# Rotating keys and queries straight from PSUM, with the head norm's factor applied afterwards on GpSimd

## The chip, the cores and the metric

One core of one Trainium2 chip. The metric is device time in microseconds of one execution of the kernel, from its start to its end. A profiled execution gives a trace besides: busy time of TensorE (PE, with its weight loads as PEld), VectorE (DVE), ScalarE (ACT), GpSimd (POOL) and the DMA queue of SyncE (SP).

## What is computed

One transformer block over 1024 latent tokens and 256 context tokens, 1024 wide: norm and modulation, a state-space branch, an attention branch with 16 query heads and 4 key/value heads of 64, a merge, and a squared-ReLU MLP. The part that matters here makes keys and queries: a projection, an RMS norm over the 64 columns of each head, the norm's weight, and a rotation by the token's row and column.

```python
def rms_norm(x, g):
    xf = x.astype(jnp.float32)
    xf = xf * lax.rsqrt(jnp.mean(xf * xf, axis=-1, keepdims=True) + NORM_EPS)
    return xf.astype(x.dtype) * g
...
q_l = apply_axial_rope(rms_norm(p_l[..., OFF_Q:OFF_K].reshape(bsz, n_tok, N_HEADS, HEAD_DIM), q_norm_g[l]), cos, sin)
k_l = apply_axial_rope(rms_norm(p_l[..., OFF_K:OFF_V].reshape(bsz, n_tok, N_KV_HEADS, HEAD_DIM), k_norm_g[l]), cos, sin)
...
k_c = rms_norm(_cols(p_c, c0, OFF_K, OFF_V).reshape(bsz, n_ctx, N_KV_HEADS, HEAD_DIM), k_norm_g[l])
```

In the rotation, the two halves of 16 columns of each axis are mixed: `x1 * cos - x2 * sin` and `x2 * cos + x1 * sin`. The norm's factor is one number for a token and a head, so it may stand before or after the rotation. Context keys (`k_c`) have no rotation.

## The kernel before

Tokens are cut into ten tiles of 128: tiles 0 to 7 latent, 8 and 9 context. Every product is made in near-float32 precision from operands split in two: `wtile` (line 124) loads a weight tile over SyncE's queue (three raw buffers), makes its high half on ScalarE (line 135) and its low half on GpSimd (line 136), with four buffers for each half. `units` (line 200) multiplies one or two token tiles with the four weight tiles of a chunk, three matmuls for each of eight pieces of the contraction (lines 210 to 212), and the third reads the low half. Its output is a PSUM tile `mm` (three buffers) or, in the wide form, alternately `mm` and `s` (three more).

The stage at issue follows the state-space branch. Keys and values come first, in the order of tiles 0 and 1 together, 2, 3, 8, 9, 4 and 5, 6 and 7 (line 1019). Then come the queries in two halves of 512 columns (eight heads each, line 1109): tiles 0 and 1 together, 2, 3, 4, 5, and 6 and 7, together in the first half and one by one in the second. Last are the values of tiles 4 to 7 (line 1131), whose place in `Vt` had been used for keys. Between the units of the second query half stand the row maxima of the first attention step (lines 1086 and 1088), two calls after each unit.

`norm_rope` (line 965) takes the PSUM tiles of one call, one or two of them. ScalarE squares each (line 974, one buffer), VectorE sums the squares by head (line 975), then makes the inverse root in a chain of 11 small operations (line 977 and `rsqrt`, lines 149 to 153), on 4, 8 or 16 columns, once for the call. Then, tile by tile, VectorE multiplies the PSUM tile with the factor into `qn` in SBUF (line 983), and makes from `qn` a product with the cosines (line 991) and two with the sines (line 996, into `t1`, one buffer). GpSimd adds the two (line 997). Context keys take one product with the norm's weight instead (line 987). The cosine and sine tables already hold the weight. After `norm_rope`, query tiles are stored to DRAM (line 1115) and read back transposed by column blocks in `qprep`; key tiles are transposed on TensorE in `k_prep` (line 1009).

In this stage no order is written out by hand: a planner orders the instructions of each engine by program order and by when it expects their inputs, and each engine's queue runs in that order. From line 1291 on, attention has a handwritten order for TensorE, VectorE, ScalarE and GpSimd.

Of the kernel before, what the change touches and what calls it, by code (L numbers as in the profile page):

```python
# [8 lines left out]
F32 = mybir.dt.float32  # L9
# [3 lines left out]
OP = mybir.AluOpType  # L13
AX = mybir.AxisListType
# [6 lines left out]
NH, NKV, HD = 16, 4, 64  # L21
# [3 lines left out]
EPS = 1e-6  # L25
# [23 lines left out]
def block_kernel(ctx, tc, io, out, dbg=None):  # L49
    nc = tc.nc  # L50
    V, S, G, T = nc.vector, nc.scalar, nc.gpsimd, nc.tensor
    LD = nc.sync
# [94 lines left out]
    def rsqrt(y, v, tmp):  # L147

        V.tensor_scalar(y.bitcast(I32), v.bitcast(I32), -0.5, 1597463007.0, op0=OP.mult, op1=OP.add)
        for _ in range(3):  # L150
            V.tensor_tensor(tmp, y, y, op=OP.mult)
            V.scalar_tensor_tensor(tmp, tmp, -0.5, v, op0=OP.mult, op1=OP.mult)
            V.scalar_tensor_tensor(y, tmp, 1.5, y, op0=OP.add, op1=OP.mult)
# [5 lines left out]
    sq = sq_.__enter__()  # L159
# [3 lines left out]
    def mmb():  # L163
        return psA.tile([128, 512], F32, name="mm", tag="mm", bufs=3)

    def six():

        cnt["n"] ^= 1
        return mmb() if cnt["n"] else psA.tile([128, 512], F32, name="s", tag="s", bufs=3)

    def trb():
        return psA.tile([128, 512], F32, name="tr", tag="tr", bufs=2)
# [12 lines left out]
    def h_l(t, k):  # L185

        f, i = (t // 4, t % 4) if t < 8 else (2, t - 8)
        return hH[f, k][:, i * 128:(i + 1) * 128], hL[f, k][:, i * 128:(i + 1) * 128]

    def chunk(c0, mid=None):  # L190

        ws = []
        for kp in range(4):
            if kp == 3 and mid:
                mid()
            src = w_in[kp * 256:(kp + 1) * 256, c0:c0 + 512].rearrange("(a p) n -> p a n", p=128)
            ws.append(wtile(src, (2, 512)))
        return ws

    def units(ws, ts, n=512, wide=False):  # L200

        pss = [(six() if wide else mmb()) for _ in ts]
        per = 8 // len(ws)
        w = 1024 // per
        for k in range(8):
            wH, wL = ws[k // per]
            o = slice((k % per) * w, (k % per) * w + n)
            for ps, t in zip([ps[:, :n] for ps in pss], ts):
                lH, lL = h_l(t, k)
                T.matmul(ps, lH, wH[:, o], start=k == 0, stop=False)  # L210
                T.matmul(ps, lL, wH[:, o], start=False, stop=False)
                T.matmul(ps, lH, wL[:, o], start=False, stop=k == 7)
        return pss
# [204 lines left out]
    for q in range(4):  # L418
# [5 lines left out]
        if q == 0:  # L424
# [6 lines left out]
            p = trb()  # L431
            for i in range(3):
# [12 lines left out]
                            op=OP.mult)  # L445
# [163 lines left out]
    for nm in ("re", "im"):  # L609
        craw = pm.tile([128, 2, 2, 128], F32, name="craw" + nm)  # L610
        src = io["ssm_c_" + nm][0].rearrange("d (o q r) h p -> d o q h r p", o=2, r=2)
# [7 lines left out]
    for nm in ("re", "im"):  # L619
        p = trb()  # L620
# [9 lines left out]
    for nm in ("re", "im"):  # L630
        b = st.tile([128, 512], F32, name="hf", tag="hf", bufs=4).rearrange("p (n h) -> p n h", h=GH)
        src = io["ssm_b_" + nm][0].rearrange("d (q r) p h -> (r p) (d q) h", r=2)
# [110 lines left out]
    for g8 in range(0, NG, 16):  # L743
        p = trb()
# [151 lines left out]
    for c in range(2):  # L896
        src = io["w_glu"][0][:, c * 256:(c + 1) * 256].rearrange("(a p) n -> p a n", p=128)
# [6 lines left out]
    for f in range(2):  # L904
        yf, gH, gL = [], [], []
        for c in range(4):
            p = trb()
            for t in range(4):
                T.transpose(p[:, t * 128:(t + 1) * 128], yld[4 * f + t][:, c * 128:(c + 1) * 128], ident)
            a = yp.tile([128, 512], F32, name="yf", tag="yf", bufs=4)  # L910
            h = yp.tile([128, 512], F32R, name="ygH", tag="ygH", bufs=5)
# [7 lines left out]
        for c in range(4):  # L919
            ps = mmb()  # L920
            wH, wL = wg[c // 2]
            prs = []
            for k in range(4):
                o = k * 256 + (c % 2) * 128
# [36 lines left out]
    rp = rp_.__enter__()  # L961
    gk = rp.tile([128, 64], F32, name="gk")
    tab = rope_tab(gk, "k_norm_g")

    def norm_rope(us, nh):

        n = nh * 64
        m = nh * len(us)
        vv = rp.tile([128, 16], F32, name="vv", tag="vv", bufs=2)[:, :m]
        yy = rp.tile([128, 16], F32, name="yy", tag="yy", bufs=2)[:, :m]  # L970
        tt = rp.tile([128, 16], F32, name="tt", tag="tt", bufs=2)[:, :m]
        for i, (ps, t, o) in enumerate(us):
            sq = rp.tile([128, 512], F32, name="sq", tag="sq", bufs=1)
            S.activation(sq[:, :n], ps[:, :n], AF.Square)
            V.tensor_reduce(vv[:, i * nh:i * nh + nh], sq[:, :n].rearrange("p (h d) -> p h d", d=64), axis=AX.X,
                            op=OP.add)
        V.tensor_scalar(vv, vv, 1.0 / HD, EPS, op0=OP.mult, op1=OP.add)
        rsqrt(yy, vv, tt)
        sh = [128, nh, 64]
        for i, (ps, t, o) in enumerate(us):  # L980
            qn = rp.tile([128, 512], F32, name="qn", tag="qn", bufs=2)
            qv = qn[:, :n].rearrange("p (h d) -> p h d", d=64)
            V.tensor_tensor(qv, ps[:, :n].rearrange("p (h d) -> p h d", d=64),
                            yy[:, i * nh:i * nh + nh, None].to_broadcast(sh), op=OP.mult)
            ov = o.rearrange("p (h d) -> p h d", d=64)
            if t >= 8:
                V.tensor_tensor(ov, qv, gk[:, None, :].to_broadcast(sh), op=OP.mult)
                continue
            cs_, sn_ = tab
            t1 = rp.tile([128, 512], F32, name="t1", tag="t1", bufs=1)  # L990
            V.tensor_tensor(ov, qv, cs_[:, t:t + 1, :].to_broadcast(sh), op=OP.mult)
            for h in range(2):
                src = qn[:, :n].rearrange("p (h a i) -> p h a i", a=2, i=32)[:, :, :, 16 * (1 - h):16 * (1 - h) + 16]
                dst = t1[:, :n].rearrange("p (h a i) -> p h a i", a=2, i=32)[:, :, :, 16 * h:16 * h + 16]
                sv = sn_[:, t:t + 1, :].rearrange("p o (a i) -> p o a i", i=32)[:, :, :, 16 * h:16 * h + 16]
                V.tensor_tensor(dst, src, sv.to_broadcast([128, nh, 2, 16]), op=OP.mult)
            G.tensor_tensor(o, o, t1[:, :n], op=OP.add)

    ws = chunk(1024)
    ksb = {}  # L1000

    def k_prep(tiles):

        c0 = tiles[0] * 128
        n = 128 * len(tiles)
        for pr_ in range(2):
            p = trb()
            for i, t in enumerate(tiles):
                T.transpose(p[:, i * 128:(i + 1) * 128], ksb[t][:, pr_ * 128:(pr_ + 1) * 128], ident)
            w = slice(c0, c0 + n)  # L1010
            ha, hb = 2 * pr_, 2 * pr_ + 1
            S.activation(KH[ha][0:64, w], p[0:64, :n], AF.Copy)
            S.activation(KH[ha][64:128, w], p[0:64, :n], AF.Copy)
            V.tensor_tensor(K2[ha][0:64, w], p[0:64, :n], KH[ha][0:64, w], op=OP.subtract)
            S.activation(KH[hb][64:128, w], p[64:128, :n], AF.Copy)
            S.activation(KH[hb][0:64, w], p[64:128, :n], AF.Copy)
            V.tensor_tensor(K2[hb][0:64, w], p[64:128, :n], KH[hb][64:128, w], op=OP.subtract)

    for ts in ([0, 1], [2], [3], [8], [9], [4, 5], [6, 7]):
        late = ts[0] in (4, 6)  # L1020
        us = []
# [20 lines left out]
    rp = rp_.__enter__()  # L1042
    gq = rp.tile([128, 64], F32, name="gq")
    tab = rope_tab(gq, "q_norm_g")
    q_d = dr.tile([8, 128, 1024], F32, name="q_d")
# [63 lines left out]
    for n in range(2):  # L1109
        ws = chunk(512 * n)  # L1110
        for ts in ([0, 1], [2], [3], [4], [5], [6, 7]) if n == 0 else ([0, 1], [2], [3], [4], [5], [6], [7]):
            us = [(ps, t, rp.tile([128, 512], F32, name="qo", tag="qo", bufs=2)) for ps, t in zip(units(ws, ts, wide=n == 0), ts)]
            norm_rope(us, 8)
            for _, t, qo in us:
                LD.dma_start(q_d[t][:, 512 * n:512 * n + 512], qo)
            if n == 0 and ts == [3]:
                k_prep((4, 5, 6, 7))
            if n == 0 and ts == [6, 7]:
                list(qprep(0))
                ms, fin = maxima(0)  # L1120
            if n == 1 and ms:
                for _ in range(2):
                    ms.pop(0)()
                if not ms:
                    list(fin())
                    list(qprep(1))
    ws = []
    for kq in range(2):
        src = w_in[kq * 512:(kq + 1) * 512, 1280:1536].rearrange("(a p) n -> p a n", p=128)
# [223 lines left out]
    def mmc():  # L1353
        return psC.tile([128, 512], F32, name="mm", tag="mm", bufs=6)
# [109 lines left out]
    def w_out_tile(n, kp):  # L1464
        src = io["w_out"][0][kp * 256:(kp + 1) * 256, n * 512:(n + 1) * 512].rearrange("(a p) n -> p a n", p=128)
        return wtile(src, (2, 512), scale_row=g1row[:, n * 512:(n + 1) * 512])
# [118 lines left out]
    for n in range(2):  # L1585
        ws = [w_out_tile(n, kp) for kp in range(4)] if n else ws_o
        for ts in ([0, 1], [2], [3], [4], [5], [6, 7]):
            pss = [mmc() for _ in ts]
            for k in range(8):
                wH, wL = ws[k // 2]  # L1590
                o = slice((k % 2) * 512, (k % 2) * 512 + 512)
# [161 lines left out]
    for bi, fts in enumerate(BL):  # L1753
        last_ = bi == NBL - 1
        tiles = (pre, pre2)[bi] if bi < 2 else [mlp2_tiles(ft) for ft in fts]
        for t in range(8):
# [4 lines left out]
            for n in range(2):  # L1761
                o = slice(n * 512, (n + 1) * 512)
                ps = mmc()
# [42 lines left out]
```

## Time and profile before

| | us |
|---|---|
| three runs, lowest, median, highest | 1907.51, 1910.69, 1912.46 |
| the profiled execution, time | 1909.88 |
| its span, first to last instruction | 1908.2 |
| TensorE busy | 1841.1 (96%) |
| VectorE busy | 1279.1 (67%) |
| GpSimd busy | 895.4 (47%) |
| ScalarE busy | 691.9 (36%) |

The time holds some 1.7 us around the span. The mean granted clock of TensorE is 0.985 of full speed. Shares over the whole span mix stages with different limits, so what a change in one stage is worth is read from that stage: from its stretch of time, and from the wait that ends last in it. The stage of keys, queries and values lies between 425 and 590.7 us.

### The profile page before, as it was taken

The numbers are of one execution on the slowest core, as the hardware profiler recorded it, in microseconds if no ns is written. First come the engines' busy times: TensorE is split into PE (matmuls) and PEld (weight loads), VectorE is DVE, ScalarE is ACT, GpSimd is POOL, SyncE is SP. The second block draws the span as 40 slices with busy tenths as digits, with TensorE's granted clock in tenths as the row PEclk, the third lists the DMA queues.
The fourth block names the chain that finished last, engine by engine and source line by source line (L and its number), as shares of the span: only waits on it lengthen the run. The fifth ranks groups of instructions, "written<-read, shape, count | busy, mean of one in ns | idle before, by whom it ended". The sixth has DMA issues, their size and how long they took to land. (4 is left out here: it accounts for less than half of the span.)

```text
span 1908.2 us, 25109 instructions
## 1 busy us (share of the span) xinstructions
PE 1841.1 (96%) x9250; PEld 1402.6 (74%) x9250; DVE 1279.1 (67%) x2194; ACT 691.9 (36%) x1016; POOL 895.4 (47%) x471
## 2 busy tenths in 40 slices
PE   7889999998999999999989999999999999999998
PEld 4668888887776556556547777887888877878887
DVE  5989998738897787777645455486454457545556
ACT  4542222244314555555442121455444541111110
POOL 2232333313425777777784453375444564443330
PEclk9989999999999999999999999999999999999999
DMA  9412222221222000000006664355554465333213
GB/s 308 97 56 71 76 77 78 76 85 46 84 71 78 18 23 23 23 23 18 22 13 207 213 209 144 116 177 182 155 155 152 126 218 178 110 107 104 89 55 144
DMA packets 179339, 200.72 MB, mean 105 GB/s; under 512 B 28112, under 2 KB 128260, under 8 KB 179216
## 3 DMA queue, kind: packets, MB, share of 16 engines
q1 hardware_dynamic: 179216, 199.11, 32.6%
q8 instruction: 73, 1.20, 0.3%
q14 instruction: 50, 0.41, 0.1%
HBM read 154.85 MB, written 44.09 MB: 104 GB/s over the span
## 5 line engine op out<-in xcount | busy, mean ns | idle before, releaser
L1202 POOL TENSOR_TENSOR accP<-accP,P 128x1024 f32<-128x1024 f32 x96 | 240.9, 2510 | 20.9 <-ACT P L1184 15.7
L1766 DVE TENSOR_TENSOR acc<-acc,mm 128x512 f32<-128x512 f32 x240 | 162.5, 686 | 127.6 <-PE mm L145 127.6
L136 POOL TENSOR_TENSOR wL<-wr,wH 128x1024 fp32r<-128x1024 f32 (+1 forms) x58 | 135.9, 2351 | 197.9 <-ACT wH L135 187.0
L1184 ACT ACTIVATE P<-sT 128x1024 f32<-128x1024 f32 x160 | 163.8, 1026 | 116.6 <-PE sT L1180 114.1
L1088 DVE TENSOR_REDUCE m<-mx 128x1 f32<-128x512 f32 x240 | 154.5, 686 | 76.1 <-PE mx L1086 69.7
L143 PE MATMUL mm<-wH,sH 128*128 128x512 f32 x480 | 187.3, 390 | 1.3 <-DVE acc L1766 1.2
L144 PE MATMUL mm<-wL,sH 128*128 128x512 f32 x480 | 186.8, 389 | 0.0
L145 PE MATMUL mm<-wH,sL 128*128 128x512 f32 x480 | 186.7, 389 | 0.0
L1197 PE MATMUL pv<-P,Vt 128*64 128x512 f32 x640 | 150.5, 600 | 0.0
L1738 POOL TENSOR_TENSOR sL<-wr,sH 128x1024 fp32r<-128x1024 f32 x30 | 72.2, 2406 | 152.0 <-ACT sH L1737 152.0
L135 ACT ACTIVATE wH<-wr 128x1024 fp32r<-128x1024 f32 (+1 forms) x62 | 61.9, 1005 | 216.2 <-PE mm L144 96.4
L1737 ACT ACTIVATE sH<-wr 128x1024 fp32r<-128x1024 f32 x30 | 31.6, 1054 | 226.5 <-issue 160.7
L1177 PE MATMUL sT<-Q,KH 128*128 128x512 f32 x320 | 105.3, 410 | 2.2 <-ACT P L1184 2.2
L143 PEld LDWEIGHTS mm<-wH,sH 128*128 128x128 f32 x480 | 90.1, 188 | 22.5 <-DVE acc L1766 2.9
L145 PEld LDWEIGHTS mm<-wH,sL 128*128 128x128 f32 x480 | 90.1, 188 | 18.9
L144 PEld LDWEIGHTS mm<-wL,sH 128*128 128x128 f32 x480 | 90.1, 188 | 18.2
L143 PE MATMUL mm<-hH,wH 128*128 128x512 f32 x248 | 101.1, 408 | 0.0
L1180 PE MATMUL sT<-Q,K 65*128 65x512 f32 x320 | 100.9, 396 | 0.0
L145 PE MATMUL mm<-hH,wL 128*128 128x512 f32 x248 | 97.7, 394 | 0.0
L144 PE MATMUL mm<-hL,wH 128*128 128x512 f32 x248 | 97.3, 392 | 0.0
L1197 PEld LDWEIGHTS pv<-P,Vt 128*64 128x64 f32 x640 | 41.7, 136 | 71.6 <-issue 62.3
L1666 POOL TENSOR_TENSOR wL<-wr,wH 128x1024 fp32r<-128x1024 f32 x32 | 76.8, 2405 | 36.6 <-ACT wH L1665 36.6
(581 smaller groups left out, 4722.8 us busy)
## 6 DMA issues: line engine op xcount, KB each, us to landing
wr<-in_w_mlp_dram SPq DMA_DIRECT2D x48, 512.0 KB
wr<-in_w_in_dram SPq DMA_DIRECT2D x35, 512.0 KB
wr<-in_w_mod_dram SPq DMA_DIRECT2D x32, 512.0 KB
s_d<-r SPq DMA_DIRECT2D x64, 256.0 KB
wr<-s_d SPq DMA_DIRECT2D x32, 512.0 KB
rw<-in_w_mlp_dram SPq DMA_DIRECT2D x30, 512.0 KB
x<-in_x_dram SPq DMA_DIRECT2D x12, 512.0 KB
xt<-in_w_mod_dram SPq DMA_DIRECT2D x24, 256.0 KB
```

The lines of the kernel that those rows point to most:

```text
L136: (low or G).tensor_tensor(L[:, :n], raw[:, :n], H[:, :n], op=OP.subtract)
L143: T.matmul(ps, lH, rH, start=i == 0, stop=False)
L144: T.matmul(ps, lH, rL, start=False, stop=False)
L145: T.matmul(ps, lL, rH, start=False, stop=i == n - 1)
L1088: V.tensor_reduce(m3[:, 4 * j + t, c:c + 1], m, axis=AX.X, op=OP.max)
L1177: T.matmul(o, KH[kv][:, ks], Q1[:, j], start=True, stop=False)
L1180: T.matmul(o, K2[kv][:, ks], Q2[:, j], start=False, stop=True)
L1184: S.activation(P, sT, AF.Exp, scale=HD ** -0.5)
L1197: T.matmul(pv[64 * j:64 * j + 64, :], Vt[:, kt, kv * 64:kv * 64 + 64], P[:, j * 512:(j + 1) * 512], start=kt == 0, stop=kt == NK - 1)
L1202: G.tensor_tensor(accP, accP, P, op=OP.add)
L1666: (low or G).tensor_tensor(L[:, :n], raw[:, :n], H[:, :n], op=OP.subtract)
L1766: V.tensor_tensor(a_, a_ if bi else bb2[:, o], ps, op=OP.add)
```

## The change

It stands in `norm_rope` and its two callers. The rotation's three products, and the one product of context keys, read the PSUM tile itself; `qn` and the pass that made it are gone. The sums of squares go into a list `pend` that is kept between calls; when it holds two token tiles, one chain makes both inverse roots, and GpSimd multiplies each rotated tile with its factor, in place. So tiles that come one by one wait for the next one. A query tile's store is issued after that multiplication. `t1` has two buffers in place of one, `qo` four in place of two.

```diff
-    def norm_rope(us, nh):
+    pend = []
+
+    def norm_rope(us, nh, done=None):
+
         n = nh * 64
-        m = nh * len(us)
-        vv = rp.tile([128, 16], F32, name="vv", tag="vv", bufs=2)[:, :m]
...
-        for i, (ps, t, o) in enumerate(us):
+        sh = [128, nh, 64]
+        for ps, t, o in us:
+            if not pend:
+                pend.append(rp.tile([128, 16], F32, name="vv", tag="vv", bufs=2))
+            i = len(pend) - 1
+            pend.append((o, t))
             sq = rp.tile([128, 512], F32, name="sq", tag="sq", bufs=1)
             S.activation(sq[:, :n], ps[:, :n], AF.Square)
-            V.tensor_reduce(vv[:, i * nh:i * nh + nh], ...)
+            V.tensor_reduce(pend[0][:, i * nh:i * nh + nh], ...)
-        V.tensor_scalar(vv, vv, 1.0 / HD, EPS, op0=OP.mult, op1=OP.add)
-        rsqrt(yy, vv, tt)
-        sh = [128, nh, 64]
-        for i, (ps, t, o) in enumerate(us):
-            qn = rp.tile([128, 512], F32, name="qn", tag="qn", bufs=2)
-            qv = qn[:, :n].rearrange("p (h d) -> p h d", d=64)
-            V.tensor_tensor(qv, ps[:, :n].rearrange("p (h d) -> p h d", d=64),
-                            yy[:, i * nh:i * nh + nh, None].to_broadcast(sh), op=OP.mult)
+            qv = ps[:, :n].rearrange("p (h d) -> p h d", d=64)
...
-            t1 = rp.tile([128, 512], F32, name="t1", tag="t1", bufs=1)
+            t1 = rp.tile([128, 512], F32, name="t1", tag="t1", bufs=2)
             V.tensor_tensor(ov, qv, cs_[:, t:t + 1, :].to_broadcast(sh), op=OP.mult)
             for h in range(2):
-                src = qn[:, :n].rearrange(...)
+                src = ps[:, :n].rearrange(...)
...
             G.tensor_tensor(o, o, t1[:, :n], op=OP.add)
+        if len(pend) < 3:
+            return
+        m = 2 * nh
...
+        V.tensor_scalar(vv, vv, 1.0 / HD, EPS, op0=OP.mult, op1=OP.add)
+        rsqrt(yy, vv, tt)
+        for i, (o, t) in enumerate(pend[1:]):
+            ov = o.rearrange("p (h d) -> p h d", d=64)
+            G.tensor_tensor(ov, ov, yy[:, i * nh:i * nh + nh, None].to_broadcast(sh), op=OP.mult)
+            if done:
+                done(o, t)
+        pend.clear()
...
-            us = [(ps, t, rp.tile([128, 512], F32, name="qo", tag="qo", bufs=2)) for ps, t in ...]
-            norm_rope(us, 8)
-            for _, t, qo in us:
-                LD.dma_start(q_d[t][:, 512 * n:512 * n + 512], qo)
+            us = [(ps, t, rp.tile([128, 512], F32, name="qo", tag="qo", bufs=4)) for ps, t in ...]
+            norm_rope(us, 8, lambda o, t: LD.dma_start(q_d[t][:, 512 * n:512 * n + 512], o))
```

## Rows read from the trace of the kernel before

**Rows 1.** Busy us by stretch, instructions in brackets; then clock, DMA share, GB/s.

```profile
480.00:513.50 33.50, 33.50 (x155) 27.82 (x154) 30.32 (x80) 11.42 (x17) 12.89 (x12) 1.00 0.17 62
513.50:530.00 16.50, 12.73 (x45) 9.98 (x44) 15.00 (x31) 3.81 (x6) 8.22 (x4) 0.79 0.42 128
530.00:580.00 50.00, 44.36 (x205) 35.31 (x205) 46.79 (x127) 9.59 (x16) 16.16 (x10) 0.98 0.23 80
580.00:590.70 10.70, 10.70 (x73) 10.70 (x74) 6.44 (x20) 0.77 (x2) 2.59 (x2) 0.78 0.59 195
sum 165.70, PE 150.38 PEld 125.02 DVE 141.33 ACT 49.12 POOL 57.89; mean PE 30.08 PEld 25.00 DVE 28.27 ACT 9.82 POOL 11.58
...
640.00:960.00 320.00, 319.52 (x1435) 188.48 (x1432) 246.26 (x328) 175.30 (x215) 235.19 (x101) 1.00 0.08 22
```

**Rows 2.** TensorE's waits, 425 to 595 us: total us, times, longest.

```profile
PE mm L212 <- POOL wL L136: 8.7, 4, 3.8
...
PE s L1086 <- DVE m L1088: 1.7, 3, 1.1
...
PE tr L1009 <- POOL ksb L997: 0.7, 1, 0.7
```

**Rows 3.** TensorE by time: start, us, line; in brackets the idling before it.

```profile
470.01 0.50 PE L212 MATMUL mm<-wL,hH 128*128 128x512 f32 x1 [2.58 <-POOL wL L136]
...
473.39 0.50 PE L210 MATMUL mm<-wH,hH 128*128 128x512 f32 x1 [0.81 <-ACT wH L135]
...
475.86 0.80 PE L212 MATMUL mm<-wL,hH 128*128 128x512 f32 x1 [1.73 <-POOL wL L136]
...
520.80 0.80 PE L212 MATMUL mm<-wL,hH 128*128 128x512 f32 x1 [3.77 <-POOL wL L136]
...
579.75 0.58 PE L210 MATMUL mm<-wH,hH 128*128 128x256 f32 x1 [2.92 <-DVE qn L983]
```

**Rows 4.** Stretches of a low granted clock, columns as in rows 1.

```profile
520.80:526.86 6.06, 6.06 (x15) 4.76 (x16) 5.82 (x8) 0.66 (x2) 4.60 (x2) 0.51 0.62 182
...
579.75:584.80 5.05, 5.05 (x23) 5.05 (x24) 4.67 (x16) 0.00 (x0) 1.29 (x1) 0.50 0.60 218
475.86:478.99 3.13, 3.13 (x7) 2.50 (x8) 2.94 (x12) 0.00 (x0) 0.00 (x0) 0.51 0.60 170
```

**Rows 5.** GpSimd by time, 505 to 519 us.

```profile
510.70 2.39 POOL L136 TENSOR_TENSOR wL<-wr,wH 128x1024 fp32r<-128x1024 f32 x1
517.18 1.26 POOL L997 TENSOR_TENSOR qo<-qo,t 128x512 f32<-128x512 f32 x1 [4.09 <-issue]
518.40 2.34 POOL L136 TENSOR_TENSOR wL<-wr,wH 128x1024 fp32r<-128x1024 f32 x1
```

**Rows 6.** VectorE by time, at 510 us.

```profile
510.80 2.33 DVE L149 TENSOR_SCALAR yy<-vv 128x8 int32<-128x8 int32 x1
```

**Rows 7.** Lines 983 and 991: ns least/median/most, first and last start, forms.

```profile
L983 DVE TENSOR_TENSOR qn<-mm,yy x17: 424/684/692, 436.8 to 584.6; 128x512 f32<-128x512 f32 x12, 128x256 f32<-128x256 f32 x5
...
L991 DVE TENSOR_TENSOR qo<-qn,cos x16: 680/688/2139, 487.0 to 585.4; 128x512 f32<-128x512 f32 x16
```

**Rows 8.** VectorE by line, 425 to 591 us: busy us, mean ns, idling before.

```profile
L152 DVE SCALAR_TENSOR_TENSOR tt<-tt,vv 128x8 f32<-128x8 f32 (+2 forms) x60 | 15.2, 253 | 1.7
```

**Rows 9.** GpSimd by line, the same stretch.

```profile
L136 POOL TENSOR_TENSOR wL<-wr,wH 128x1024 fp32r<-128x1024 f32 x11 | 26.5, 2421 | 18.4 <-PE s L212 10.9 <-ACT wH L135 7.4
L997 POOL TENSOR_TENSOR qo<-qo,t 128x512 f32<-128x512 f32 x16 | 21.7, 1353 | 65.2 <-DVE t L996 27.1 <-issue 18.1 <-DVE tt L151 8.0
```

**Rows 10.** Waits of SyncE's queue, 425 to 595 us.

```profile
SPq L1115 <- POOL qo L997: 82.8, 16, 12.4
```

**Rows 11.** ScalarE's waits, the same stretch.

```profile
ACT sq L974 <- DVE vv L975: 18.8, 6, 9.1
```

More of the change, by code (lines that the diff above doesn't have):

```diff
@@ L963, in block_kernel @@
     tab = rope_tab(gk, "k_norm_g")
-    def norm_rope(us, nh):
+    pend = []
+    def norm_rope(us, nh, done=None):
         n = nh * 64
-        m = nh * len(us)
-        vv = rp.tile([128, 16], F32, name="vv", tag="vv", bufs=2)[:, :m]
-        yy = rp.tile([128, 16], F32, name="yy", tag="yy", bufs=2)[:, :m]
-        tt = rp.tile([128, 16], F32, name="tt", tag="tt", bufs=2)[:, :m]
-        for i, (ps, t, o) in enumerate(us):
+        sh = [128, nh, 64]
[4 more added lines that the diff above has]
+            pend.append((o, t))
             sq = rp.tile([128, 512], F32, name="sq", tag="sq", bufs=1)
             S.activation(sq[:, :n], ps[:, :n], AF.Square)
-            V.tensor_reduce(vv[:, i * nh:i * nh + nh], sq[:, :n].rearrange("p (h d) -> p h d", d=64), axis=AX.X,
+            V.tensor_reduce(pend[0][:, i * nh:i * nh + nh], sq[:, :n].rearrange("p (h d) -> p h d", d=64), axis=AX.X,
                             op=OP.add)
-        V.tensor_scalar(vv, vv, 1.0 / HD, EPS, op0=OP.mult, op1=OP.add)
-        rsqrt(yy, vv, tt)
-        sh = [128, nh, 64]
-        for i, (ps, t, o) in enumerate(us):
-            qn = rp.tile([128, 512], F32, name="qn", tag="qn", bufs=2)
-            qv = qn[:, :n].rearrange("p (h d) -> p h d", d=64)
-            V.tensor_tensor(qv, ps[:, :n].rearrange("p (h d) -> p h d", d=64),
-                            yy[:, i * nh:i * nh + nh, None].to_broadcast(sh), op=OP.mult)
+            qv = ps[:, :n].rearrange("p (h d) -> p h d", d=64)
             ov = o.rearrange("p (h d) -> p h d", d=64)
@@ L989, in norm_rope @@
             cs_, sn_ = tab
-            t1 = rp.tile([128, 512], F32, name="t1", tag="t1", bufs=1)
+            t1 = rp.tile([128, 512], F32, name="t1", tag="t1", bufs=2)
             V.tensor_tensor(ov, qv, cs_[:, t:t + 1, :].to_broadcast(sh), op=OP.mult)
             for h in range(2):
-                src = qn[:, :n].rearrange("p (h a i) -> p h a i", a=2, i=32)[:, :, :, 16 * (1 - h):16 * (1 - h) + 16]
+                src = ps[:, :n].rearrange("p (h a i) -> p h a i", a=2, i=32)[:, :, :, 16 * (1 - h):16 * (1 - h) + 16]
                 dst = t1[:, :n].rearrange("p (h a i) -> p h a i", a=2, i=32)[:, :, :, 16 * h:16 * h + 16]
@@ L997, in norm_rope @@
             G.tensor_tensor(o, o, t1[:, :n], op=OP.add)
+        if len(pend) < 3:
+            return
+        m = 2 * nh
+        vv = pend[0][:, :m]
+        yy = rp.tile([128, 16], F32, name="yy", tag="yy", bufs=2)[:, :m]
+        tt = rp.tile([128, 16], F32, name="tt", tag="tt", bufs=2)[:, :m]
+        V.tensor_scalar(vv, vv, 1.0 / HD, EPS, op0=OP.mult, op1=OP.add)
[6 more added lines that the diff above has]
+        pend.clear()
     ws = chunk(1024)
@@ L1111, in block_kernel @@
         for ts in ([0, 1], [2], [3], [4], [5], [6, 7]) if n == 0 else ([0, 1], [2], [3], [4], [5], [6], [7]):
-            us = [(ps, t, rp.tile([128, 512], F32, name="qo", tag="qo", bufs=2)) for ps, t in zip(units(ws, ts, wide=n == 0), ts)]
-            norm_rope(us, 8)
-            for _, t, qo in us:
-                LD.dma_start(q_d[t][:, 512 * n:512 * n + 512], qo)
+            us = [(ps, t, rp.tile([128, 512], F32, name="qo", tag="qo", bufs=4)) for ps, t in zip(units(ws, ts, wide=n == 0), ts)]
+            norm_rope(us, 8, lambda o, t: LD.dma_start(q_d[t][:, 512 * n:512 * n + 512], o))
             if n == 0 and ts == [3]:
```

## Prediction

> **What bounds the kernel now.** I first read the busy time by stretch over the stage that the change touches, the projections of keys and queries with their head norm and rotation, 425 to 590.7 us [rows 1]. TensorE is the engine that sets the pace before and after: from 640 to 960 us, in attention, it is busy 319.5 of 320 us. Inside the stage it is not: from 480 to 513.5 us it is full, but from 513.5 to 530 it works 12.7 of 16.5 us and from 530 to 580 44.4 of 50, and there VectorE is the busier engine, with 15.0 of 16.5 and 46.8 of 50 us. At 590.7 us TensorE goes into attention with no gap, so a microsecond that it loses in this stage is one that the end loses, and one given back is given back in full, as long as attention's own inputs are there. The question is therefore how much TensorE loses here, and whether the change reaches it.
>
> Second view: whom TensorE waited for [rows 2]: 8.7 us in four waits for the low half of a weight (line 136, on GpSimd), 1.7 us for VectorE's row maxima (line 1088), 0.7 us for a rotated key row (line 997). Third: the rows of its waits in order of time [rows 3]. There are five that matter: 2.58, 0.81 and 1.73 us at 467 to 476 us (first half of the query weights), 3.77 us at 517 us (second half), 2.92 us at 577 us, where a PSUM buffer was held until line 983 had read it. Fourth: the granted clock behind the long ones [rows 4]. Behind three of them TensorE ran at 0.50 or 0.51, its lower level of 1.2 GHz, for 3.13, 6.06 and 5.05 us; half of each, 1.5, 3.0 and 2.5 us, is loss as well. Sum of what TensorE can get back: waits 8.7 + 1.7 + 0.7 + 0.81 + 2.92 = 14.8 us, clock 7.0 us, together 21.8 us. That is the ceiling.
>
> Fifth, the cause of the largest. At 517 us the second low half stood in GpSimd's queue behind the rotation add of a query tile (line 997), which began at 517.18 us after 4.09 us of idling, because VectorE was late; the low halves ran from 518.40 us on [rows 5]. VectorE was late for two reasons: it has that much to do, and the port. Its small operation of line 149 began at 510.80 us and took 2.33 us, until the low half begun on GpSimd at 510.70 us with 2.39 us had ended [rows 5, 6]. That one is no exception: line 991, with both inputs in SBUF, takes 688 ns in the median and up to 2139 ns; line 983, which does the same amount of work with one input in PSUM, takes 684 ns and never more than 692 ns [rows 7]. So here a VectorE operation on SBUF alone can be held for a whole GpSimd instruction and one that reads PSUM is not.
>
> **Part 1: the normalising pass goes.** 16 passes over 512 columns at 0.684 us and 10 over 256 at 0.424 us [rows 7]: 10.9 + 4.2 = 15.2 us less on VectorE.
>
> **Part 2: roots for two tiles.** There were 20 chains of 11 small operations (7 for keys, 13 for queries). Now there are 5 + 8 = 13. 7 x 11 = 77 operations fewer at the 0.253 us that line 152 takes on average, waits for the port included [rows 8]: 19.5 us less.
>
> **Part 3: the rotation reads PSUM.** The count of operations is the same. Price of one: 0.684 us by line 983 (PSUM) and 0.688 by line 991 (SBUF) [rows 7], so nothing; that the runs of 16 columns in the sine products cost more from PSUM is not shown, and I bound it by 0 and by 0.1 us for each of 52 products, 5 us of VectorE time. A gain on the other side: the products no longer read two SBUF inputs, and the excess of line 991, a maximum of 2.14 against 0.69 us, goes. I take nothing for both. A rule speaks against this part: the Trainium skill, VectorE: DVE Perf Modes, section Rules for kernel authors, advises to copy matmul output from PSUM to SBUF first if many operations follow. By it the three PSUM reads should be dearer than one read and two in SBUF; the two medians above say that for float32 here they are not. For the other effect the rows come first as well (688 ns with 2139 at most, against 684 with 692); the Trainium skill, SBUF — State Buffer, section SBUF: two separate sides, calls the pair of ports that VectorE and GpSimd share an exclusive lock, taken by VectorE operations with two SBUF inputs among others, and the rows agree.
>
> Together VectorE loses some 35 us of work (15.2 + 19.5), of 141 us in the stage. From 530 to 580 us seven tiles lose 0.69 + 5.5 x 0.253 = 2.1 us each, 14.6 us: 46.8 becomes 32 of 50 us, well below TensorE's 44.4 [rows 1]. VectorE stops being the bound there.
>
> **Part 4: GpSimd takes the factor.** 16 multiplications of 512 columns at the add's 1.353 us [rows 9] and 10 of half that, by the same row 0.68: 21.6 + 6.8 = 28.4 us more. The inner broadcast of the factor is not in the trace; I take the add's price, with the low half's 2.42 us for 1024 columns, 1.21 for 512, as the lower end and twice the add's (2.7 us) as the upper. GpSimd has the room: 58 us of 166 are busy now. The order of its queue is what counts. The planner places the multiplications, and each waits for VectorE's chain of 11; whatever stands behind a waiting one waits too, and among it are the low halves of the weights. Each pair has two multiplications, 2.7 us; there are three trains of low halves (the two halves of the query weights, the value weights). If one of the three is pushed back by a whole pair, that is 2.7 us of TensorE waiting; none would be 0, all three 8.1. I take 2.7, since the chain now begins sooner than the whole rotation did.
>
> **Part 5: later stores.** The store of the first tile of a pair now waits for the second tile. SyncE's queue already waits 82.8 us in 16 stores [rows 10], and behind such a store stand loads of weights. A load that comes later costs at most a wait like the present 3.77 us. At the end, 10.7 us of value projections on a full TensorE [rows 1] cover the last pair's chain (11 x 0.253 = 2.8 us), its two multiplications (2.7 us) and store. I take 0.
>
> **Which waits go, and what is late next.** Key row, 0.7 us: the roots of tiles 2 and 3 are one chain instead of two in a row; gone, 0.7. First query weights, 2.58 + 0.81 + 1.73 + 1.5 of clock = 6.6 us: two causes. The low halves stood behind an add that waited for VectorE, and ScalarE's squares waited 18.8 us in all, once 9.1 us, for VectorE's sums (line 975) because there is one square buffer [rows 11]; the fourth weight's high half stood behind that. But the first low half can't start before TensorE has freed one of its four buffers, which the change doesn't touch. I take 4.0 of 6.6. Second query weights, 3.77 + 3.0 = 6.8: the add that was in front now comes directly behind the rotation; next comes TensorE's own need, and I take 6.0. Maxima, 1.7: I take 1.4. PSUM buffer, 2.92 + 2.5 = 5.4: the buffer is free after the rotation, without the chain, and VectorE has no backlog; 5.0. The last 0.6 us of the 8.7 (value weights) stays. Sum 0.7 + 4.0 + 6.0 + 1.4 + 5.0 = 17.1 us, less 2.7 for GpSimd's queue: 14.4 us.
>
> **Rival A: GpSimd becomes the gate.** In all three trains the multiplications stand ahead of low halves. For: the queue is in order, and while GpSimd works without a pause VectorE's small operations get through one at a time (2.33 us for one). Against: GpSimd is idle for two thirds of the stage. Then what VectorE itself gave goes through (maxima 1.4, PSUM buffer 5.0, key row 0.7), the weight waits stay: 7.1 us, less some 2: 1905 us.
>
> **Rival B: slower, by GpSimd's queue.** The same mechanism, past the point where it only keeps the old waits: a low half that ends later than now. It decides as soon as the second low half of a train ends after TensorE has used up the first, and it feeds itself, since each low half holds one of the 11 small operations and the multiplication behind them holds the next low half. A train of four then pays one wait like the present one, with clock, 6.8 us. Two trains more than now, 13.6, less 7.1: 6.5 us slower, 1917 us. It would need multiplications at the upper price.
>
> **Rival C: nothing.** The planner's new order on the four engines outside the handwritten order gives up about what the waits gave back, or the multiplication costs 2.7 us: 1906 to 1912, say 1909 us.
>
> **How the numbers follow.** The profiled execution took 1909.9 us, its span 1908.2; the median of the runs is 1910.7, 0.8 more. 1909.9 - 14.4 = 1895.5; on the median 1896.3. I forecast 1896 us. Its own range goes from the ceiling, 1910.7 - 21.8 = 1889, to 1903. Chances: forecast 0.58, rival A 0.18, rival C 0.13, rival B 0.11. A measurement of this kernel tells about 0.3%, 5.7 us, from no change: the bound is 1905. Rival A lies on it; I count half of it as faster. Faster 0.58 + 0.10 = 0.68, same 0.08 + 0.13 = 0.21, slower 0.11. The range that leaves out rival B and what lies beyond the ceiling is 1888 to 1910.
>
> **What would show it.** In the changed profile: no group on the old line 983; from 530 to 580 us or its like VectorE busy near 65% instead of 94%; 28 us more on GpSimd; the rotation never longer than some 0.75 us for 512 columns; TensorE's wait of 3.77 us and the one of 2.92 us gone, with the half clock behind them; attention's start some 14 us sooner than 590.7 us, and the distance from there to the end unchanged. The forecast is wrong if TensorE waits longer for low halves on GpSimd than the 8.7 us it does now, if the multiplication costs far more than 1.35 us, or if attention starts sooner but the time behind it grows.

## The result

The changed kernel takes 1893.4 us in the median of four runs (1886.0 to 1895.4), beside 1911.3 us before. The ratio is 0.9899, 95% interval 0.9872 to 0.9927, so 17.9 us are gained and between 14 and 24 are consistent with the runs. The forecast was 1896 us (1888 to 1910), faster.

Line numbers in the changed kernel: 978 the square, 979 its sum, 988 the product with the cosines, 993 those with the sines, 994 the add on GpSimd, 1001 and 149 to 153 the chain of the inverse root (1001 first, then 149), 1005 the factor on GpSimd.

The stage first. Its start is put at the same work in each kernel, 62.2 us after the last matmul of the state-space loop starts, which is 440 us before and 437.4 us after; its end is attention's first score matmul (591.1 and 568.1 us). Busy time by stretch, with the columns of [rows 1]. First the kernel before, over the whole stage, which the earlier rows gave in parts:

```profile
440.00:591.10 151.10, 135.78 (x664) 112.97 (x663) 133.40 (x361) 40.82 (x71) 53.73 (x38) 0.94 0.25 83
```

and the changed kernel:

```profile
437.40:568.10 130.70, 127.65 (x664) 107.90 (x663) 101.02 (x260) 41.21 (x72) 73.03 (x63) 1.00 0.28 95
```

The stage went from 151.1 to 130.7 us, 20.4 us less. TensorE's idling fell from 151.1 - 135.8 = 15.3 to 130.7 - 127.65 = 3.05 us, and the granted clock rose from 0.94 to 1.00, so that the same 664 matmul records take 127.65 instead of 135.78 us. That is 12.3 us less of waits and 8.1 us less of matmul time; some 7 of the 8.1 are the three stretches of half clock in [rows 4]. VectorE is busy 101 instead of 133 us, GpSimd 73 instead of 54.

What TensorE still waits for in the stage, in total and by time:

```profile
PE mm L212 <- POOL wL L136: 3.0, 3, 1.3
```

```profile
464.57 0.50 PE L212 MATMUL mm<-wL,hH 128*128 128x512 f32 x1 [0.97 <-POOL wL L136]
468.31 0.50 PE L212 MATMUL mm<-wL,hH 128*128 128x512 f32 x1 [0.70 <-POOL wL L136]
...
557.74 0.39 PE L212 MATMUL mm<-wL,hH 128*128 128x256 f32 x1 [1.29 <-POOL wL L136]
```

Against [rows 2, 3]: the 3.77 us at the second query half, the 2.92 us for the PSUM buffer, the wait for the key row and those for the maxima are gone; three short ones for low halves are left. No stretch of a lower clock follows any of them (1.00 over the whole stage), where the kernel before had three [rows 4].

### The profile page after: what moved, and what is told of

Read it like the earlier page. It is cut to its first block, busy times and chain, and to the rows that moved or that the text cites. A ratio compares the mean times of both kernels' runs of the same rounds, so it can differ in the third digit from the quotient of the medians.

```text
span 1883.9 us, 25028 instructions
## 1 busy us (share of the span) xinstructions
PE 1832.2 (97%) x9250; PEld 1396.6 (74%) x9250; DVE 1242.9 (66%) x2091; ACT 692.2 (37%) x1016; POOL 914.3 (49%) x497
## 3 DMA queue, kind: packets, MB, share of 16 engines
q1 hardware_dynamic: 179216, 199.11, 32.4%
## 4 chain that ended last, share of the span: by engine, by line
PE 70%; issue 10%; POOL 8%; DVE 7%; DMA 2%; ACT 2%; SPq 0%; POOLq 0%; DVEq 0%; ACTq 0%
PE mm L143 11%; PE mm L145 11%; PE mm L144 11%; PE pv L1206 7%; POOL wL L1675 5%; PE sT L1186 4%; PE sT L1189 4%; PE mx L1097 3%; PE s L859 2%; PE mm L210 1%; PE mm L1603 1%; PE mm L1605 1%; PE mm L212 1%; PE mm L1604 1%; PE mm L211 1%
## 5 line engine op out<-in xcount | busy, mean ns | idle before, releaser
L1211 POOL TENSOR_TENSOR accP<-accP,P 128x1024 f32<-128x1024 f32 x96 | 239.9, 2499 | 21.6 <-ACT P L1193 16.4
L136 POOL TENSOR_TENSOR wL<-wr,wH 128x1024 fp32r<-128x1024 f32 (+1 forms) x58 | 135.8, 2348 | 182.7 <-ACT wH L135 182.7
L135 ACT ACTIVATE wH<-wr 128x1024 fp32r<-128x1024 f32 (+1 forms) x62 | 62.1, 1005 | 216.4 <-PE mm L144 83.6
```

The lines of the kernel that those rows point to most:

```text
L136: (low or G).tensor_tensor(L[:, :n], raw[:, :n], H[:, :n], op=OP.subtract)
L1211: G.tensor_tensor(accP, accP, P, op=OP.add)
```

## The experiments

In each, the number to compare is the length of the stage, cut as above: 151.1 us before, 130.7 after. It is far steadier than the whole time: the one repetition of the same kernel has it within 0.1 us (e8), while the times of one kernel differ by up to 12 us between runs. The stage of each, in one line of the stretch view per kernel, stands with it. "Idling" below is the stretch less TensorE's busy time.

**The shared chain alone (e1).** The kernel before, with the sums kept until two tiles are there; the rest of `norm_rope` then runs over both. The change's four `qo` buffers come with it.

```diff
-    def norm_rope(us, nh):
+    pend = []
+    def norm_rope(us, nh, done=None):
...
+        if len(pend) < 3:
+            return
+        m = 2 * nh
+        vv = pend[0][:, :m]
+        us = pend[1:]
...
         for i, (ps, t, o) in enumerate(us):
             qn = rp.tile([128, 512], F32, name="qn", tag="qn", bufs=2)
```

> Only the shared chain: the kernel before, with one chain of inverse roots for two token tiles; the normalising pass stays on VectorE ahead of the rotation, GpSimd gets no factor. The stage from 440 us to attention took 151.1 us before and 130.7 us after. Theory L (load: what counts is how much work leaves VectorE, whichever it is): VectorE loses 7 chains, 15 to 19 us of the 34, so the stage shortens by at least half of the 20.4 us, to 141 us or less, and the time is some 1900. Theory C (coupling: what counts is that rotation, add and PSUM buffer no longer wait for the chain, and that products from PSUM can't be held by GpSimd): adds and buffers now wait for two tiles and the chain, so the weight waits behind the adds stay or grow, the stage is 146 us or more and the time 1906 or more.

```profile
438.10:582.00 143.90, 133.09 (x664) 111.64 (x663) 115.19 (x286) 41.37 (x71) 55.06 (x38) 0.96 0.26 87
```

143.9 us, 7.2 us less than before, between the bounds of the two theories; the time is 1902.4 us against 1909.2 (ratio 0.9961, 0.9942 to 0.998). VectorE lost the 18 us that seven chains cost, but TensorE still waits 5.6 us for low halves, and once 3.6 us for VectorE's maxima.

**No shared chain (e2).** The changed kernel with a chain per call.

```diff
-        if len(pend) < 3:
-            return
-        m = 2 * nh
+        m = (len(pend) - 1) * nh
```

> The changed kernel without the shared chain: a chain for each call again (20 of them), the rotation still from PSUM and the factor still on GpSimd. VectorE gets back 7 chains, 15 to 19 us. Theory L: as in the run with the shared chain alone, about half of the gain is left, stage 139 to 142 us, time 1901 to 1904. Theory C: nearly all of the gain stays, stage 131 to 135 us, time 1894 to 1897; VectorE stays below TensorE's work and its chain holds only the multiplications.

```profile
438.70:576.30 137.60, 130.46 (x665) 108.80 (x664) 119.28 (x338) 41.31 (x72) 73.10 (x63) 0.99 0.27 90
```

137.6 us, again between the bounds: 6.9 us longer than the changed kernel; time 1898.2 us (0.9932, 0.9912 to 0.9953).

**The factor on VectorE (e3).**

```diff
-            G.tensor_tensor(ov, ov, yy[:, i * nh:i * nh + nh, None].to_broadcast(sh), op=OP.mult)
+            V.tensor_tensor(ov, ov, yy[:, i * nh:i * nh + nh, None].to_broadcast(sh), op=OP.mult)
```

> The changed kernel with the factor applied by VectorE instead of GpSimd, still on rotated rows: VectorE gets back 26 passes, 15 us, and GpSimd loses its 23 us. Theory L: half of the gain, stage about 140 us, 1902 us. Theory C: most of the gain, 131 to 135 us; TensorE's remaining waits for low halves (3.0 us after) go towards 0 if GpSimd's multiplications cause them, and stay at 3 if the square, sum and rotation do.

```profile
438.10:575.10 137.00, 130.65 (x664) 110.28 (x663) 119.19 (x289) 41.64 (x72) 51.56 (x37) 0.98 0.27 91
```

137.0 us, 6.3 us longer; time 1894.4 us (0.9916, 0.9891 to 0.9941). The waits for low halves fell from 3.0 to 2.0 us, but TensorE now waits 1.7 us for a high half (line 135 on ScalarE) and 2.6 us for VectorE's maxima.

What e1 to e3 say together: the shared chain (e2) and the factor's move to GpSimd (e3) are each worth 6 to 7 us of stage on top of the rest of the change, and the shared chain alone is worth 7.2. Load alone (theory L) doesn't order them: e1 has the least work on VectorE, 115.2 us against 119.3 and 119.2, and the longest stage. Coupling alone (theory C) doesn't either, for putting 18 us of work back on VectorE cost 6 to 7 us where it had said 1 to 4. Both count, and neither theory alone had these times.

**The buffers alone (e4).**

```diff
-            t1 = rp.tile([128, 512], F32, name="t1", tag="t1", bufs=1)
+            t1 = rp.tile([128, 512], F32, name="t1", tag="t1", bufs=2)
...
-            us = [(ps, t, rp.tile([128, 512], F32, name="qo", tag="qo", bufs=2)) for ps, t in ...]
+            us = [(ps, t, rp.tile([128, 512], F32, name="qo", tag="qo", bufs=4)) for ps, t in ...]
```

> The kernel before with the change's buffers alone: two for the sine products, four for the query rows. A rival says that part of the gain is these buffers: VectorE waited 4.0 us for GpSimd to release the one sine buffer. By that, the stage would be 147 us or less. I expect 150 to 152 us and a time within 2 us of before, since VectorE's lateness is set by its work and the port.

```profile
438.20:588.50 150.30, 134.31 (x665) 111.81 (x663) 136.53 (x363) 40.69 (x72) 53.33 (x38) 0.95 0.25 83
```

150.3 us and a ratio of 1.0004 (0.9991 to 1.0017): the buffers are not where the gain comes from.

**Rotation from an SBUF copy (e5), and the copy with no reader (e9).** ScalarE copies the PSUM tile; in e5 the products read the copy, in e9 they read PSUM as in the changed kernel.

```diff
+            qn = rp.tile([128, 512], F32, name="qn", tag="qn", bufs=2)
+            S.activation(qn[:, :n], ps[:, :n], AF.Copy)
-            qv = ps[:, :n].rearrange("p (h d) -> p h d", d=64)
+            qv = qn[:, :n].rearrange("p (h d) -> p h d", d=64)
...
-                src = ps[:, :n].rearrange(...)
+                src = qn[:, :n].rearrange(...)
```

> The changed kernel, but ScalarE first copies each PSUM tile to SBUF (26 copies, 13 us on ScalarE) and VectorE's products read that copy, so they have two SBUF inputs again; shared chain and factor on GpSimd as in the changed kernel. VectorE's operations and their number are the same. If only VectorE's work counts, the stage stays at 131 to 133 us (130.7 in the changed kernel) and the time at 1893 to 1896. If being held by GpSimd counts (products of 0.69 us that take up to 2.14), the maximum of a product goes from 0.69 back to some 2 us and the stage to 135 us or more.

> The changed kernel with the same 26 copies on ScalarE as in the run that rotates from SBUF, but nothing reads them: the products read PSUM as in the changed kernel. It takes the copies' own cost (13 us of ScalarE, a PSUM tile kept until it is copied) apart from what two SBUF inputs cost. That run's stage was 146.8 us, the changed kernel's 130.7. If being held by GpSimd made the difference, this one takes 131 to 134 us. If the copies did, in ScalarE's queue or by keeping the PSUM tile, it takes 140 us or more.

The stage of e5, then of e9:

```profile
437.60:584.40 146.80, 131.94 (x666) 110.50 (x665) 123.94 (x266) 51.25 (x95) 79.03 (x63) 0.98 0.26 85
```

```profile
439.30:570.20 130.90, 127.55 (x664) 107.86 (x663) 101.66 (x262) 51.11 (x95) 73.47 (x63) 1.00 0.28 95
```

146.8 against 130.9 us: 15.9 of the 20.4 us are lost again when the products have two inputs in SBUF, and none by the copies themselves. The times say the same, 1907.5 us (0.9978, 0.9964 to 0.9992) against 1893.5 (0.9902, 0.9884 to 0.992). Where they went is in VectorE's groups (busy us, mean ns), of e5:

```profile
L995 DVE TENSOR_TENSOR t<-qn,sin 128x256 f32<-128x256 f32 (+1 forms) x44 | 32.4, 770 | 0.7 <-POOL sin L957 0.7
L990 DVE TENSOR_TENSOR qo<-qn,cos 128x512 f32<-128x512 f32 x16 | 18.1, 1134 | 3.7 <-POOL cos L952 3.7
```

and of the changed kernel, where the sine products stand in two groups by the PSUM tile they read, of which this is the larger:

```profile
L993 DVE TENSOR_TENSOR t<-mm,sin 128x256 f32<-128x256 f32 (+1 forms) x30 | 10.6, 388 | 0.6 <-POOL sin L957 0.6
...
L988 DVE TENSOR_TENSOR qo<-mm,cos 128x512 f32<-128x512 f32 x12 | 8.2, 684 | 3.8 <-POOL cos L952 3.7
```

A sine product takes 770 instead of 388 ns, a cosine product 1134 instead of 684. GpSimd pays too: e5's factor takes 1189 ns in the mean where the changed kernel's takes 1046. The schedules are nearly the same: between e5 and e9 GpSimd's queue differs in a single place, ScalarE's in none, VectorE's in two and TensorE's in three, and VectorE never waits for one of e5's copies. With that, TensorE's wait for low halves is back at 10.0 us:

```profile
PE mm L212 <- POOL wL L136: 10.0, 4, 3.3
```

What holds them is seen in e5's rows by time, VectorE and then GpSimd:

```profile
510.71 3.74 DVE L995 TENSOR_TENSOR t<-qn,sin 128x256 f32<-128x256 f32 x2
```

```profile
511.65 7.87 POOL L136 TENSOR_TENSOR wL<-wr,wH 128x1024 fp32r<-128x1024 f32 x3
```

The second of these two products begins at 511.90 us, behind the first low half, takes 2.56 us and ends 0.28 us after that low half does. The Trainium skill, SBUF — State Buffer, section SBUF: two separate sides, calls the port pair that the two engines share an exclusive lock held for a whole instruction, taken by VectorE operations with two SBUF inputs among others. The trace agrees, and the 15.9 us between e5 and e9 are what it costs here.

It is not mainly the factor that holds them. Over e5's stage the products take some 27 us more than at their shortest (an estimate: each one's time less a short one of its form), against 6 in the kernel before; about 13 of the 27 lie beside low halves, 8 beside the factor and 5 beside adds.

**The norm's result written back to PSUM (e10).** Is that price already paid in the kernel before?

```diff
-            qn = rp.tile([128, 512], F32, name="qn", tag="qn", bufs=2)
+            qn = ps
```

> The kernel before with one change: the normalising pass writes its result back into the PSUM tile instead of an SBUF tile, so the three products read one input from PSUM. Same operations on every engine, the same 20 chains, the same order of norm and rotation, no factor on GpSimd; the PSUM tile is kept three products longer. Only what a second SBUF input costs is taken away. If that is a cause of its own in the kernel before, its products no longer exceed 0.7 us (2.14 at most before), and the stage falls from 151.1 us by what they and GpSimd lost, 4 us or more, to 147 us or less. If it counts only once the factor is on GpSimd, the stage stays at 149 to 152 us.

```profile
437.70:589.00 151.30, 136.62 (x665) 114.58 (x664) 131.60 (x362) 40.82 (x71) 51.52 (x38) 0.93 0.26 82
```

151.3 us, the same as before; ratio 1.0003 (0.9989 to 1.0017). The products are indeed no longer held: line 991 takes 692 ns at most, where [rows 7] show 2139. But most of what they no longer lose the chain loses instead. Line 151 in e10, busy us and mean ns:

```profile
L151 DVE TENSOR_TENSOR tt<-yy 128x8 f32<-128x8 f32 (+2 forms) x57 | 17.1, 300 | 1.5
```

and in the kernel before:

```profile
L151 DVE TENSOR_TENSOR tt<-yy 128x8 f32<-128x8 f32 (+2 forms) x57 | 13.5, 236 | 1.6
```

And TensorE waits 3.3 and 3.0 us for PSUM buffers until the last product has read them, where it waited 2.9 us for line 983. So reading PSUM is worth nothing on balance in the old order, with the longer hold on the PSUM tile in that balance, and 15.9 us in the order of the changed kernel.

**A dearer factor (e6).**

```diff
+    one_ = cst.tile([128, 512], F32, name="one_")
+    V.memset(one_, 1.0)
...
             G.tensor_tensor(ov, ov, yy[:, i * nh:i * nh + nh, None].to_broadcast(sh), op=OP.mult)
+            G.tensor_tensor(o, o, one_, op=OP.mult) if nh == 8 else G.tensor_tensor(o, o, one_[:, :256], op=OP.mult)
```

> The changed kernel with a second multiplication (by ones) behind each factor on GpSimd, 1.29 us for a query tile: together 2.3 us, near the upper price that the prediction gave the factor (2.7). GpSimd gets 28 us more, 101 of 131 us. Rival B of the prediction says that at this price low halves come later than before the change: TensorE's wait for them over 8.7 us, with clock the stage at 145 us or more. The theory that GpSimd has slack, since its multiplications stand where it idled, says 133 to 137 us, waits for low halves 4 to 8 us.

```profile
438.70:581.10 142.40, 132.78 (x665) 111.54 (x664) 112.58 (x262) 41.75 (x72) 99.54 (x89) 0.96 0.26 88
```

142.4 us, between the two ranges, so neither expectation held; time 1903.2 us (0.9958, 0.9942 to 0.9973). The wait for low halves is 8.6 us, as much as before the change:

```profile
PE mm L212 <- POOL wL L136: 8.6, 4, 3.0
```

That is the prediction's rival A, the old weight waits with the VectorE part of the gain kept, and it stands at twice the price that the factor has. The slower outcome, rival B, is not reached there.

**Two low halves on VectorE (e7).** What the trace of the changed kernel offers next.

```diff
-    def chunk(c0, mid=None):
+    def chunk(c0, mid=None, low=()):
...
-            ws.append(wtile(src, (2, 512)))
+            ws.append(wtile(src, (2, 512), low=V if kp in low else None))
...
-        ws = chunk(512 * n)
+        ws = chunk(512 * n, low=(2,) if n == 0 else ())
...
-        ws.append(wtile(src, (4, 256)))
+        ws.append(wtile(src, (4, 256), low=V if kq else None))
```

> The changed kernel with two low halves moved from GpSimd to VectorE, which now idles: the third weight tile of the first query half and the second of the value weights. Of TensorE's three remaining waits, 3.0 us, these two head 0.97 and 1.29 us. I expect both gone and the third (0.70 us) gone or the same: stage 128 to 129 us, 1.5 to 3 us less than the changed kernel. A rival: VectorE's low half is held by GpSimd's, or delays sums and squares, and the stage stays at 130 to 132 us.

```profile
438.10:565.30 127.20, 127.11 (x666) 107.97 (x665) 101.92 (x264) 41.52 (x72) 70.68 (x61) 1.00 0.29 98
```

127.2 us, with TensorE busy 127.1: no wait is left in the stage, and this is what its matmuls need at the full clock. That is 3.5 us less than the changed kernel, a little more than expected, and the third wait is gone too. The time is 1887.5 us (0.987, 0.9855 to 0.9885), the fastest of all here, 3.4 us below e8 on the same chip. The stage is 3.4 us shorter as well. The intervals of the two ratios overlap; the rows of the stage don't leave it in doubt there.

**The changed kernel again (e8).**

> The changed kernel once more, beside the others on the same chip: is the 20.4 us of the stage in one profiled execution repeated, and how much of the run's difference lies outside? I expect the stage at 130 to 132 us and the time 15 to 21 us below the kernel before; what the first profile showed besides (2.6 us at the start, 1.3 us behind attention's start) has no place in the code and should come and go.

```profile
438.10:568.70 130.60, 127.53 (x664) 107.90 (x663) 101.42 (x262) 41.57 (x72) 73.56 (x63) 1.00 0.29 95
```

130.6 us; time 1890.9 us against 1911.1, ratio 0.9898 (0.9877 to 0.9918). The stage repeats. What the first profile showed besides is only partly there: its stage started 2.6 us sooner than before (1.9 here; 437.4 and 438.1 against 440), and from attention to the end it took 1315.8 us where the kernel before took 1317.1 and this run 1317.6. Over all profiles that stretch, which no edit touches, takes 1314.5 (e3) to 1323.8 us (e5), and that is why the stage is the better measure. Most of the unchanged starts lie near 438 in the other experiments too, so the first 2 us belong to the one profile of before and not to the change.

## Why the prediction was right

**What bounds.** That a microsecond of TensorE in this stage is one of the end held: 20.4 and 20.5 us of stage in two profiles, 17.9 and 20.2 us in the medians; in the other nine experiments too the median moved by what the stage did, within 2.5 us. The ceiling was set too low, at 21.8 us: e7 reaches 151.1 - 127.2 = 23.9. The clock was priced rightly: the three low stretches add up to 7.1 us, and the granted clock is 1.00 in the rest of the stage. The other 1.0 of the 8.1 us less of matmul time goes with the number of waits (TensorE is busy 127.1 us in e7, with none, and 127.65 with three); why is not shown. The rest is small waits that the list left out.

**Parts 1 and 2, less work on VectorE.** Forecast 15.2 and 19.5 us. Putting a pass per tile or the seven chains back (e3, e2) adds 18.2 and 18.3 us to VectorE's busy time. Those are not clean prices: e3's passes take 14.1 us, at 687 ns each for 512 columns, and the rest is small operations of the chains that are held longer. Together 34.7 was forecast; the stage shows 133.4 - 101.0 = 32.4. From 530 us on VectorE was to be busy near 65%:

```profile
530.00:570.00 40.00, 38.71 (x218) 33.14 (x218) 26.92 (x71) 10.18 (x17) 17.26 (x13) 1.00 0.34 120
```

26.9 of 40 us is 67%, and was 94% [rows 1].

**Part 3, the PSUM reads.** The price, nothing, was right: line 988 takes 684 ns in the mean, and a sine product of 256 columns 414 in the median. The other half of this part was the one mis-sized term that matters: "I take nothing for both" put down as zero that products from PSUM can't be held. By e5 and e9 it is 15.9 us of the stage. (With e2's 6.9 and e3's 6.3 that is more than the whole gain: each is measured with the other two in place.) The size could not be read from the kernel before, and e10 shows why: there it is worth 0 on balance. Why it is dear in the new order is shown in part. In the old order GpSimd's add waits for the products of its own tile [rows 9], and 8 of the stage's 68 products meet a GpSimd instruction; in e5 34 do, low halves, factors and adds, and the products are held 27 us instead of 6. GpSimd's new work is 8 of the 27. No run has the products read SBUF with the factor on VectorE, so what the new order does alone and what the factor adds stays open.

That the time came out near the forecast is here in part luck. The sum has no term for this: it would have given the same 1896 us for e5, which takes 1907.5. The chip was near because the change happened to contain what the sum left out.

**Part 4, the factor on GpSimd.** Forecast at the add's 1.353 us. It takes less:

```profile
L994 POOL TENSOR_TENSOR qo<-qo,t 128x512 f32<-128x512 f32 x16 | 20.6, 1295 | 16.4 <-DVE vv L1001 10.3 <-issue 4.3 <-DVE t L993 1.8
L1005 POOL TENSOR_TENSOR qo<-qo,yy 128x512 f32<-128x512 f32 x16 | 16.4, 1046 | 18.4 <-DVE yy L153 18.4
```

1.046 us with the second input broadcast along the head, less than the lower end of my bound (1.21). 16.4 + 3.6 + 2.4 = 22.4 us in the stage instead of 28.4. That GpSimd's queue would cost 2.7 us was close in size, 3.0 us of waits for low halves. But I counted it twice: those 3.0 us are mostly what is left of the old waits, and the list had already left more than that, 21.8 - 17.1 = 4.7 us, before the 2.7 came off.

**Part 5.** SyncE's queue waits 53.8 us in 16 stores, not 82.8 [rows 10], and no engine waits for a load of weights in the stage.

**The waits one by one.** First query weights: 4.0 of 6.6 us forecast, 5.0 gone (0.97 + 0.70 are left, without low clock). Second: 6.0 of 6.8, all gone. PSUM buffer: 5.0 of 5.4, all gone. Maxima: 1.4 of 1.7, all gone, with 0.4 that I had not listed. Key row: 0.7, gone. Value weights: no change forecast, 0.6 became 1.3. Each was taken a little low and the 2.7 us came off on top; that is why the sum was 14.4 and the stage gave 20.4.

**The rivals.** Rival A is real, and e6 finds it at 2.3 us for a factor; with 1.05 it stays away. Rivals B and C did not come. The chip was inside the range, and 3 us below the forecast.

## What to carry to other kernels

Before work moves from VectorE to GpSimd, look at what VectorE does meanwhile: products with two SBUF inputs were held here until a GpSimd instruction ended (2.56 us for one of 0.4), those with one input in PSUM never (692 ns at most), so let VectorE read PSUM while GpSimd takes the SBUF-to-SBUF pass. The worth of that can't be read from the kernel without the move; test the two together. And when a wait has vanished, subtract the new queue's cost only from what is left of it.

## What the runs showed of the hardware

A GpSimd multiplication whose second input is one number per head, broadcast along 64 columns, takes 1046 ns for 128x512, an add of two full tensors 1295. It is the broadcast and not the operation: e6's multiplication by a full tensor takes 1295 too.

The small operations of the root chains bear what is left of the holding. In the changed kernel's stage, lines 149 and 152, on 8 or 16 columns:

```profile
L149 DVE TENSOR_SCALAR yy<-vv 128x16 int32<-128x16 int32 (+1 forms) x12 | 12.2, 1019 | 0.4
L152 DVE SCALAR_TENSOR_TENSOR tt<-tt,vv 128x16 f32<-128x16 f32 (+1 forms) x36 | 12.1, 337 | 1.1
```

Line 149 takes 1019 ns in the mean and 171 ns at least. Of its 12 runs nine are held by an add on GpSimd and two by a low half, some 10 us in all; line 152 is held up to 2311 ns. One input in SBUF is enough for line 149 to be held, while the sum of line 979, which also reads SBUF alone, never takes more than 0.69 us. TensorE's few waits show that the holding now lies beside its work.
